# Two transformer blocks on one core: attention's products a stage later, earlier bias rows and squares, the last norm without GpSimd

## The chip, the core and the metric

The kernel runs on one core of a Trainium2 chip. The metric is device time of one execution in microseconds (us). The engines are named as the profile names them: PE (TensorE; PEld is its weight loads), DVE (VectorE), ACT (ScalarE), POOL (GpSimd) and SP (SyncE, which here issues nearly all DMAs).

## The reference

256 tokens of width 1024, fp32, go through two different transformer blocks and a last norm:

```python
# block 1
h = token_mixer(rmsnorm(x, norm_mix_pre), w_in, ...)      # four groups of 4 heads x 64:
#   mLSTM, short convolution, MoBA attention (one block of 256 keys: causal, with a relative bias),
#   HGRN2; head norms and gates; then y @ w_out
x = x + rmsnorm(h, norm_mix_post)
x = x + rmsnorm(memory_cross_attention(rmsnorm(x), rmsnorm(mem, mem_norm), ...))
x = x + rmsnorm(conv_glu_ffn(rmsnorm(x), ...))
# block 2
h = x + hybrid_mixer(rmsnorm_2(x, norm_mix), ...)  # 8 "fox" heads (causal, with a decay), 8 NSA heads
#   (compressed, selected and window branch), each 512 wide, up-projected, gated, summed, @ w_out
h = h + peer_ffn(rmsnorm_2(h, norm_ffn), ...)      # 16,384 single-neuron experts, top 16 of 8 heads
return rmsnorm_2(h, norm_final)                    # h * rsqrt(mean(h*h) + 1e-6) * norm_final
```

## The kernel before, in words

**Products.** The activations lie as features x tokens. Every weight and every activation is split into a high half (ACT copies it, L370) and a low half (the difference: DVE, or POOL for every so many weights, L328), and each product is three matmuls into one PSUM tile: `mm3`, L346 to 351, so that L349, L350 and L351 are the lines of nearly all of PE's work. `whalf` (L319) loads 512 KB of weights on SP's queue and makes both halves; four buffers of each are there. `fm_pair` makes 256 output features (48 matmuls), `fm_quad` (L390) two such pairs at once. PSUM has four tiles `acc` and four `att`.

**Order.** The program is written out stage by stage; a scheduler then orders each engine's instructions, except in pieces marked as ordered by hand. `behind()` and `issue_after` only add a constraint. Small attention work is written as generators, which `step()` or `next()` moves on by one stage between the big projections.

**Attention** (`attention`, L1673) is used three times: MoBA in block 1 (2 steps of two heads), fox (4 steps) and NSA (8 steps) in block 2. `scores` puts q·k and the biases into PSUM, ACT takes the exponentials, DVE the maxima, the sums' reciprocals and the scaling (L1710), and the result is `attP`. `values` transposes it on PE (L1718), ACT copies it to `attPT`, and PE multiplies it by v (L1726). A stage is: the scores of step j+1, then transposes and products of step j.

**Block 1's mixer** (L1354) makes the projections one by one and advances `moba`, `lstm` (mLSTM, L1532; two stages for each half c of the heads) and `memory` (keys and values of the memory, `memory_kv`, L649) between them. MoBA's bias comes from small tables: `cst1` and `bk` are loaded (L1513, L1514), a matmul (L1517) makes the rows `dr`, which go to DRAM and come back as the Toeplitz tile `toep` (L1522). Each half of mLSTM and HGRN2 ends in a `head_norm` (L555): square on ACT, a matmul for the means (L562), Ln and Exp on ACT, three DVE steps (`newton`, L450 to 452), a product with the gate on POOL (L567) and one on DVE (L569) into `y`. `y` is split into `yh` and `yl`, two of its eight rows of features at a time, and the mixer's output projection (`fm_quad` with the order 6, 7, 2, 3, 4, 5, 0, 1) multiplies those; rows 0 and 1 are mLSTM's. The memory's norm sums (squares on ACT, DVE additions, a matmul L470) are asked for by its first pair of projections.

**Block 2** (L762). `rotated` (L925) projects, rotates (a matmul, L864) and advances fox by one stage; `merge(j)` (L944) makes the gates' projections, one for each NSA stage. Between them lies a small softmax over compressed keys (L975 to L977), transposed at L981.

**Last norm** (L1312 to 1352, DVE and ACT ordered by hand). Two halves of 128 tokens by two halves of 512 features. `square` adds the last products (L1316), squares on ACT with a row sum and multiplies by the weights on POOL (L1319). `rms` and `newton` make the factor of a token half; `store` multiplies by it (DVE, L1337; ACT for the last quarter) and issues the DMA (three on SP, the last on ACT, L1338).

Of the kernel before, what the change touches and what calls it, by code (L numbers as in the profile page):

```python
# [15 lines left out]
AF = mybir.ActivationFunctionType  # L16
# [276 lines left out]
class Normed:  # L293


    def __init__(self, x, hi, lo):
        self.x, self.halves, self.r, self.rc, self.first = x, (hi, lo), None, None, None


class Prog:  # L300
# [68 lines left out]
    def act(self, out, in_, f, **k):  # L369
        return self.nc.scalar.activation(out, in_, f, **k)  # L370
# [83 lines left out]
    def norm_sums(self, n):  # L454

        if n.r is not None:
            return
        nc, x = self.nc, n.x
        s = None
        for p in range(4):  # L460
            sq = self.npool.tile([128, 2, T], F32, tag="sq" if s is not None else "sums", name="sq", bufs=3 if s is not None else 1)
            i = self.act(sq, x[:, 2 * p:2 * p + 2], AF.Square)
            if s is None:
                s = sq
                table = self.lntable(i)
            else:
                nc.vector.tensor_add(s, s, sq)
        ms = self.att((128, T))
# [180 lines left out]
    def memory_kv(self, pool, mem, km, vm):  # L649

        n = Normed(mem, *[pool.tile([128, 8, T], F32R, tag="mn" + t, name="mn" + t) for t in "hl"])
        self.norm_sums(n)
        self.gain_halves(n, self.v("mem_norm"))
        yield
        for j in range(2):
            ps = self.fm_norm(n, after=None)
            self.act(km[:, 2 * j:2 * j + 2].rearrange("p a b -> p (a b)"), ps, AF.Copy)
            yield
        ps = self.tm(n.halves, 512, self.plast)
        for b in range(2):  # L660
            self.act(vm[:, b], ps[b], AF.Identity, scale=self.cols(n, b))
# [100 lines left out]
    def block2(self, n):  # L762
# [4 lines left out]
        with tc.tile_pool(name="b2", bufs=1) as bp:  # L767
# [8 lines left out]
            with tc.tile_pool(name="b2a", bufs=1) as ap:  # L776
# [148 lines left out]
                def rotated(dst, scale):  # L925
                    r = rope(fl(dst), self.fm_pair(n.halves), T, c2("cosT"), c2("sinT"), scale)
                    next(r)
                    next(fox, None)
                    next(r, None)
                    next(cmp)  # L930
# [9 lines left out]
                for _ in fox:  # L940
                    pass
# [15 lines left out]
                merge(0)  # L957

# [19 lines left out]
                merge(1)  # L978
                pt = self.att((128, 2, 128))
# [3 lines left out]
                for j in range(2, 8):  # L983
                    next(nsa, None)
                    merge(j)
                for _ in nsa:
                    pass
                mr = self.npool.tile([128, 8, T], F32, tag="hg", name="mr")
                mh, ml = [ap.tile([128, 8, T], F32R, tag=t, name=t) for t in ("fqk", "knq")]
                for m_, y in ((0, yf), (1, yn)):  # L990
                    yh = ap.tile([128, 2, 4, T], F32R, tag="LR"[m_] + "T", name="yh")
                    for j in range(2):
                        self.split(yh[:, 0, 2 * j:2 * j + 2], yh[:, 1, 2 * j:2 * j + 2], y[:, 2 * j:2 * j + 2])
                    y = yh[:, 0], yh[:, 1]
                    for j in range(4):
                        ps = self.fm_pair(y, nk=4)
# [171 lines left out]
    def peer(self):  # L1168
# [7 lines left out]
        with ExitStack() as es:  # L1176
# [137 lines left out]

            def square(b, n):
# [17 lines left out]
            def store(b, n):  # L1333
                if b and n:
                    act(half[b][n], half[b][n], AF.Identity, scale=r[b])
                else:
                    nc.vector.tensor_scalar(half[b][n], half[b][n], r[b], None, op0=ALU.mult)  # L1337
                (nc.scalar if b and n else nc.sync).dma_start(self.out[b * 128:(b + 1) * 128, n * 512:(n + 1) * 512], half[b][n])  # L1338

            with tc.manual_schedule(engines={mybir.EngineType.DVE, mybir.EngineType.Activation}):  # L1340
                square(0, 0)
                square(0, 1)
                rms(0)
                square(1, 0)
                newton(0)
                square(1, 1)
                store(0, 0)
                store(0, 1)
                rms(1)
                newton(1)  # L1350
                store(1, 0)
                store(1, 1)

    def block1_mixer(self, n, first):  # L1354
# [4 lines left out]
        with tc.tile_pool(name="mix", bufs=1) as mp:  # L1359
# [143 lines left out]
            mq = proj("m_q")  # L1503
            mk = proj("m_k", 0.125, hb[:, 4:6])
            aq = proj("a_q", 0.125, hb[:, 6:8])
            ak = proj("a_k")
            values(512, 768)
            step(levels)

# [12 lines left out]
            nc.sync.dma_start(toep, bass.AP(tensor=dr.tensor, offset=dr.offset, ap=[[1, 128], [384, 4], [1, T]]))  # L1522

# [10 lines left out]
            def mlstm():  # L1534
                W = mp.tile([128, 4, 384], F32, tag="mW", name="mW")
                for c in range(2):
# [17 lines left out]
                    pn, pd, pm = [self.att((128, T)) for _ in range(3)]  # L1554
# [5 lines left out]
                    mm(pm, sel[:, 2 * c:2 * c + 2].rearrange("p h d -> p (h d)"), g4[:, 4], start=True, stop=True)  # L1560
                    em = v2("em")[:, :1]
# [31 lines left out]
            step(moba)  # L1593
# [25 lines left out]
            cc = proj("c_c")  # L1619
            step(lstm)  # L1620
# [4 lines left out]
            self.table = self.htable  # L1625
# [47 lines left out]
    def attention(self, pool, npair, q, k, v, bias, out, nsa=None):  # L1673
# [5 lines left out]

        nc, mm = self.nc, self.nc.tensor.matmul  # L1680
# [32 lines left out]
        def values(P, ch, br):  # L1713
# [7 lines left out]
            first = None  # L1721
            for blk in range(2):
                for i in (1, 0):
# [4 lines left out]
                    first = first or m  # L1728
# [3 lines left out]
        P = scores(*steps[0])  # L1732
        yield
        for j, step in enumerate(steps):
            p = step[0] // 2
            last, P = P, scores(*steps[j + 1]) if j + 1 < len(steps) else None
            if j % per == 0:
                po = self.acc((128, 2, T))
                if nsa:
                    for c in range(2):  # L1740
                        nsa[1](po, c, 2 * p + c)
            values(last, *step)
            if j % per == per - 1:
                nc.vector.tensor_copy(out[:, 2 * p:2 * p + 2], po)
            yield
# [22 lines left out]
```

## Time and profile before

| what | us |
|---|---|
| three runs: median (lowest to highest) | 1486.6 (1484.2 to 1488.93) |
| the profiled execution's own time | 1486.23 |
| its span, first to last instruction | 1484.5 |
| PE busy | 1439.0 (97%) |
| DVE busy | 1081.2 (73%) |
| ACT busy | 782.6 (53%) |
| POOL busy | 227.6 (15%) |
| mean granted TensorE clock | 0.995 of full speed |

The page gives busy times as shares of the span. PE's share hides its waits, which stand in the timeline of its instructions as "[idle before <-releaser]". By its timeline the stages are: block 1's mixer to about 180 us, the cross attention to about 270, the FFN, block 2's mixer from about 455 to 650, expert retrieval to 760, the experts to 1471, and the last norm.

### The profile page before, as it was taken

To read this page: it belongs to the slowest core of one execution; us is meant where nothing else is said; L and a number is where in the kernel's file an instruction comes from. 1 tells how busy PE (TensorE), PEld (TensorE's weight loads), DVE (VectorE), ACT (ScalarE), POOL (GpSimd) and SP (SyncE) were. 2 spreads that over 40 slices of the span, in tenths; PEclk is the share of its full clock that TensorE was granted. 3 is DMA by queue.
4 is the path that set the end of the run, shared out by engine and by line. 5 is a ranking of instruction groups with operands and counts; after the bars stand their busy time and mean duration, and the time that the engine had idled before them with its cause. 6 is when DMAs were issued, how large, how long until landed. Compare 5 with 4: busy or idle time off the path is not lost.

```text
span 1484.5 us, 26777 instructions
## 1 busy us (share of the span) xinstructions
PE 1439.0 (97%) x10614; PEld 1335.9 (90%) x10614; DVE 1081.2 (73%) x1994; ACT 782.6 (53%) x1314; POOL 227.6 (15%) x143
## 2 busy tenths in 40 slices
PE   8899898999999999999899999999999999999997
PEld 7789888999999889999899999999998888888886
DVE  7768687766777655579988888778887555655555
ACT  7446466444556756556444545544445455455454
POOL 3731000222200431106441220000000000000001
PEclk9999999999999999999999999999999999999999
DMA  6443332555555423464355545545446555655553
GB/s 245 149 158 127 126 117 93 176 175 185 194 172 176 157 90 125 128 199 164 122 183 163 167 157 185 166 162 170 159 167 217 197 192 192 198 194 191 196 191 123
DMA packets 68245, 246.64 MB, mean 166 GB/s; under 512 B 7540, under 2 KB 8568, under 8 KB 67864
## 3 DMA queue, kind: packets, MB, share of 16 engines
q1 hardware_dynamic: 67544, 243.10, 50.0%
q8 instruction: 83, 1.36, 0.4%
q10 hardware_dynamic: 576, 1.84, 0.3%
q14 instruction: 42, 0.34, 0.1%
HBM read 242.80 MB, written 2.10 MB: 165 GB/s over the span
## 4 chain that ended last, share of the span: by engine, by line
PE 74%; DVE 10%; ACT 2%; issue 1%; POOL 0%; ACTq 0%; DVEq 0%
PE acc L349 20%; PE acc L350 20%; PE acc L351 19%; PE att L350 3%; PE att L351 3%; PE att L349 3%; PE att L1240 2%; DVE wl L328 1%; DVE uvl L1094 1%; DVE tmp L1016 1%; PE att L1691 1%; PE acc L1726 1%; ACT wh L370 1%; DVE ti L1019 1%; DVE ti L1018 1%
## 5 line engine op out<-in xcount | busy, mean ns | idle before, releaser
L1094 DVE TENSOR_TENSOR uvl<-uv,uvh 128x1024 fp32r<-128x1024 f32 x234 | 291.7, 1247 | 153.9 <-ACT uvh L370 153.7
L370 ACT ACTIVATE uvh<-uv 128x1024 fp32r<-128x1024 f32 x256 | 270.2, 1057 | 237.0 <-PE acc L350 133.4
L370 ACT ACTIVATE wh<-w 128x1024 fp32r<-128x1024 f32 x187 | 195.9, 1056 | 200.9 <-PE acc L350 104.0
L351 PE MATMUL acc<-hh,uvl 128*128 128x256 f32 x1024 | 289.8, 283 | 5.3 <-DVE uvl L1094 4.3
L349 PE MATMUL acc<-hh,uvh 128*128 128x256 f32 x1024 | 294.2, 287 | 0.1
L350 PE MATMUL acc<-hl,uvh 128*128 128x256 f32 x1024 | 289.9, 283 | 0.0
L328 DVE TENSOR_TENSOR wl<-w,wh 128x1024 fp32r<-128x1024 f32 x146 | 184.6, 1272 | 76.6 <-ACT wh L370 76.0
L351 PEld LDWEIGHTS acc<-hh,uvl 128*128 128x128 f32 x1024 | 196.0, 191 | 6.1 <-DVE uvl L1094 4.9
L350 PE MATMUL acc<-uvl,ch 128*128 128x512 f32 x512 | 199.2, 389 | 0.0
L351 PE MATMUL acc<-uvh,cl 128*128 128x512 f32 x512 | 199.2, 389 | 0.0
L349 PEld LDWEIGHTS acc<-hh,uvh 128*128 128x128 f32 x1024 | 196.0, 191 | 0.3 <-ACT uvh L370 0.3
L350 PEld LDWEIGHTS acc<-hl,uvh 128*128 128x128 f32 x1024 | 196.1, 192 | 0.0
L349 PE MATMUL acc<-xnh,wh 128*128 128x256 f32 x544 | 156.9, 289 | 4.6 <-ACT wh L370 3.2
L328 POOL TENSOR_TENSOR wl<-w,wh 128x1024 fp32r<-128x1024 f32 x41 | 101.0, 2464 | 369.1 <-ACT wh L370 362.2
L351 PE MATMUL acc<-xnh,wl 128*128 128x256 f32 x544 | 155.0, 285 | 1.7 <-POOL wl L328 1.0
L350 PE MATMUL acc<-xnl,wh 128*128 128x256 f32 x544 | 155.4, 286 | 0.2
L349 PE MATMUL acc<-uvh,ch 128*128 128x512 f32 x512 | 138.5, 389 | 0.0
L349 PEld LDWEIGHTS acc<-uvh,ch 128*128 128x128 f32 x512 | 96.1, 188 | 20.0
L350 PEld LDWEIGHTS acc<-uvl,ch 128*128 128x128 f32 x512 | 96.1, 188 | 19.9
L351 PEld LDWEIGHTS acc<-uvh,cl 128*128 128x128 f32 x512 | 96.1, 188 | 19.9
L349 PEld LDWEIGHTS acc<-xnh,wh 128*128 128x128 f32 x544 | 104.2, 192 | 8.1 <-ACT wh L370 4.5
L350 PE MATMUL att<-xnl,wh 128*128 128x256 f32 x368 | 104.5, 284 | 2.9 <-DVE xnl L545 2.9
(433 smaller groups left out, 2959.3 us busy)
## 6 DMA issues: line engine op xcount, KB each, us to landing
w<-in_W_dram SPq DMA_DIRECT2D x188, 512.0 KB, 4.4
uv<-in_U_dram SPq DMA_DIRECT2D x128, 512.0 KB, 3.6
uv<-in_V_dram SPq DMA_DIRECT2D x128, 512.0 KB, 3.6
mg<-in_cw_dram SPq DMA_DIRECT2D x4, 512.0 KB, 7.2
x<-in_xT_dram SPq DMA_DIRECT2D x2, 512.0 KB, 5.4
mem<-in_memT_dram SPq DMA_DIRECT2D x1, 1024.0 KB, 6.6
sk<-in_W_dram SPq DMA_DIRECT2D x1, 1024.0 KB, 6.3
xd<-xt SPq DMA_DIRECT2D x2, 512.0 KB, 2.6
```

Source lines behind the costliest of these rows:

```text
L328: (self.nc.gpsimd if pool else self.nc.vector).tensor_tensor(out=lo, in0=w, in1=hi.bitcast(F32), op=ALU.subtract)
L349: mm(ps, wsl(w[0]), xsl(x[0]), start=first, stop=False, **k)
L350: mm(ps, wsl(w[0]), xsl(x[1]), start=False, stop=False, **k)
L351: self.last_mm = mm(ps, wsl(w[1]), xsl(x[0]), start=False, stop=last, **k)
L370: return self.nc.scalar.activation(out, in_, f, **k)
L1016: nc.vector.match_replace(tmp[:, :n], vals[:, 0:8], src, -3.0e38)
L1018: nc.vector.max_index(idx[:, 0:8], vals[:, 0:8], src)
L1019: nc.vector.max_index(idx[:, 8:16], vals[:, 8:16], tmp[:, :n])
L1094: i = (nc.gpsimd if lo_pool else nc.vector).tensor_tensor(out=lo, in0=w, in1=hi.bitcast(F32), op=ALU.subtract)
L1240: mm(ps[:, j], m1[:, j], m2[:, s * NT + j], start=s == 0, stop=s == 1)
L1691: m = mm(S[i][:, part[blk]], q[rows[i], ch, blk * 128:(blk + 1) * 128], k[rows[i], br if nsa else ch, :128 * (blk + 1)], start=blk == 1, s ...
L1726: m = mm(po[rows[i], ch % 2, 128 * blk:], v[:, blk, vc:vc + 64], PT[i][:, 256 * blk:256 + 128 * blk], start=not nsa and blk == 0, stop=blk ...
```

## The change

**Attention.** `values` is cut in two: `turn` transposes and copies, `values` multiplies. A stage now is either "products of step j-1, then scores of step j+1" or "transposes of step j", so a step takes two stages, and its products come behind the next step's scores. The callers step twice where they stepped once; the small softmax's transposes are moved behind `merge(2)`, and the last NSA stages go between the up-projections.

```diff
-        def values(P, ch, br):
+        def turn(P):
             PT = []
...
                 self.act(PT[i], pt, AF.Copy)
-            first = None
+            return PT
+
+        def values(PT, ch, br):
+            first = self.last_mm
...
-        for j, step in enumerate(steps):
-            p = step[0] // 2
+        for j in range(len(steps) + 1):
+            if j:
+                p = steps[j - 1][0] // 2
+                if j % per == 1:
+                    po = self.acc((128, 2, T))
...
+                values(PT, *steps[j - 1])
+                if j % per == 0:
+                    nc.vector.tensor_copy(out[:, 2 * p:2 * p + 2], po)
+            if j == len(steps):
+                return
             last, P = P, scores(*steps[j + 1]) if j + 1 < len(steps) else None
-            if j % per == 0:
...
-            values(last, *step)
...
+            yield
+            PT = turn(last)
             yield
```

**Block 1.** The bias rows (L1511 to 1522) stand ahead of the projections `m_q` to `a_v` instead of behind them. The memory's squares are cut out of `norm_sums` and asked for at the start of `memory_kv`; its sums are finished in mLSTM's second half. Two of mLSTM's PSUM tiles become one.

```diff
     def memory_kv(self, pool, mem, km, vm):
-        self.norm_sums(n)
+        self.squares(n)
         self.gain_halves(n, self.v("mem_norm"))
+        self.mem = n
...
-                    pn, pd, pm = [self.att((128, T)) for _ in range(3)]
+                    pq = self.att((128, 2, T))
+                    pn, pd = pq[:, 0], pq[:, 1]
+                    pm = self.att((128, T))
...
+                    if c:
+                        self.table = self.htable
+                        self.norm_sums(self.mem)
```

**Last norm.** The multiplication by the weights moves from POOL to DVE, for three of the four quarters, between the additions, into rows of a buffer that is free by then (`og`). The last quarter is stored by one DVE instruction that multiplies by both; ACT scales two quarters.

```diff
-                nc.gpsimd.tensor_tensor(out=half[b][n], in0=half[b][n], in1=gn[:, n * 512:(n + 1) * 512], op=ALU.mult)
+            def gained(b, n):
+                nc.vector.tensor_mul(og[b][n], half[b][n], gh[n])
...
+            def store(b, n, scalar):
+                o = og[b][n]
+                if scalar:
+                    act(o, o, AF.Identity, scale=r[b])
+                elif b and n:
+                    nc.vector.scalar_tensor_tensor(o, half[b][n], r[b], gh[n], op0=ALU.mult, op1=ALU.mult)
                 else:
+                    nc.vector.tensor_scalar(o, o, r[b], None, op0=ALU.mult)
```

PE and SP have as many instructions as before, DVE 2 more, ACT 1 more, POOL 4 fewer. Three places show the new order; line numbers are each kernel's own (1751 and 1762 are the new 1718 and 1726, 569 the new 562).

PE at the end of block 1's mixer (`yh`, `yl` the halves of `y`; `sq` mLSTM's squares, `attP` and `attPT` MoBA's), before:

```order
L351 MATMUL acc<-yh,wl 128x256
L562 MATMUL att<-sq,bd_128 128x256
L1718 MATMUL att<-ident,attP 128x128 x6
L1726 MATMUL acc<-attPT,vt 64x256 x2
L1726 MATMUL acc<-attPT,vt 64x128 x2
L349 MATMUL acc<-yh,wh 128x256 x2
L350 MATMUL acc<-yl,wh 128x256
```

and now (the two matmuls of L349 in one row are the first of rows 0 and 1 for both pairs there, as in the row above):

```order
L349 MATMUL acc<-yh,wh 128x256
L350 MATMUL acc<-yl,wh 128x256
L569 MATMUL att<-sq,bd_128 128x256
L351 MATMUL acc<-yh,wl 128x256
L349 MATMUL acc<-yh,wh 128x256 x2
L350 MATMUL acc<-yl,wh 128x256
```

MoBA's transposes and products are gone from between the head norm's matmul and the rows of `y` that come out of that head norm; they stand earlier.

PE in block 2 at the first fox step, before:

```order
L834 MATMUL att<-maskb,identb 128x128
L1718 MATMUL att<-ident,attP 128x128 x6
L864 MATMUL att<-raw,cst_5049 128x256 x2
L1726 MATMUL acc<-attPT,vt 64x256 x2
L1726 MATMUL acc<-attPT,vt 64x128 x2
L349 MATMUL acc<-xnh,wh 128x256
```

and now, around the first of the two groups of transposes (L1751; the products, L1762, stand 30 rows further down, behind the scores of the next step):

```order
L349 MATMUL acc<-xnh,wh 128x256
L872 MATMUL att<-raw,cst_5047 128x256 x2
L1751 MATMUL att<-ident,attP 128x128 x3
L350 MATMUL acc<-xnl,wh 128x256
L351 MATMUL acc<-xnh,wl 128x256
```

Big matmuls stand between scores, transposes and products, which followed each other directly before.

DVE at the end of the program (`fin` the result, `fss` and `fr` the sums and factors of a token half), before:

```order
L1316 TENSOR_TENSOR fin<-fin,acc 128x512
L1329 SCALAR_TENSOR_TENSOR fss_16431<-fss_16431,fr_16433 128x1
L1330 TENSOR_SCALAR fss_16431<-fss_16431 128x1
L1331 TENSOR_TENSOR fr_16433<-fss_16431,fr_16433 128x1
L1316 TENSOR_TENSOR fin<-fin,acc 128x512
L1337 TENSOR_SCALAR fin<-fin,fr_16433 128x512 x2
L1322 TENSOR_TENSOR fss_16432<-fss_16432 128x1
```

and now:

```order
L1334 TENSOR_TENSOR fin<-fin,acc 128x512
L1338 TENSOR_TENSOR buf_8313<-fin,gn 128x512
L1334 TENSOR_TENSOR fin<-fin,acc 128x512
L1348 SCALAR_TENSOR_TENSOR fss_16429<-fss_16429,fr_16431 128x1
L1349 TENSOR_SCALAR fss_16429<-fss_16429 128x1
L1350 TENSOR_TENSOR fr_16431<-fss_16429,fr_16431 128x1
L1341 TENSOR_TENSOR fss_16430<-fss_16430 128x1
L1343 TENSOR_SCALAR fss_16430<-fss_16430 128x1
L1359 TENSOR_SCALAR buf_8313<-buf_8313,fr_16431 128x512
```

The sums of the second token half (`fss_16430`) stand ahead of the first store; before, two stores stood ahead of them.

## Rows read from the trace of the kernel before

**Rows 1.** The page: busy us, share of the span and instructions of each engine.

```profile
PE 1439.0 (97%) x10614; PEld 1335.9 (90%) x10614; DVE 1081.2 (73%) x1994; ACT 782.6 (53%) x1314; POOL 227.6 (15%) x143
```

**Rows 2.** Timeline of PE in block 1: start us, us, instruction, [idle before <-releaser].

```profile
92.33 1.55 PE L1525 MATMUL att<-toep,cst 128*128 128x256 f32 x8 [0.88 <-DMA toep<-dr]
...
107.94 0.44 PE L1609 MATMUL att<-hA,vt 128*64 128x128 f32 x4 [1.52 <-ACT attPT L370]
...
152.54 0.39 PE L349 MATMUL acc<-yh,wh 128*128 128x256 f32 x1 [0.95 <-ACT km L370]
...
155.52 0.59 PE L562 MATMUL att<-sq,bd 128*128 128x256 f32 x2
...
157.80 0.87 PE L1726 MATMUL acc<-attPT,vt 128*64 128x256 f32 x8 [1.03 <-ACT attPT L370]
...
160.12 0.50 PE L349 MATMUL acc<-yh,wh 128*128 128x256 f32 x2 [1.46 <-ACT yh L370]
...
160.85 0.39 PE L350 MATMUL acc<-yl,wh 128*128 128x256 f32 x1 [0.22 <-DVE yl L341]
...
161.07 0.28 PE L351 MATMUL acc<-yh,wl 128*128 128x256 f32 x1
...
161.19 0.28 PE L349 MATMUL acc<-yh,wh 128*128 128x256 f32 x1
```

**Rows 3.** Windows: stretch, us, busy us (instructions) per engine, PEclk, DMA share, GB/s.

```profile
160.00:165.00 5.00, 4.65 (x24) 4.45 (x25) 1.49 (x3) 0.70 (x2) 0.00 (x0) 0.66 0.00 0
...
205.00:215.00 10.00, 7.34 (x40) 6.07 (x39) 7.20 (x13) 4.53 (x14) 0.00 (x0) 0.89 0.50 161
...
250.00:260.00 10.00, 6.46 (x46) 5.96 (x47) 8.01 (x15) 5.95 (x11) 2.13 (x1) 1.00 0.28 88
...
500.00:530.00 30.00, 28.26 (x279) 24.32 (x278) 19.20 (x42) 15.18 (x43) 11.72 (x8) 1.00 0.44 152
```

**Rows 4.** Timeline of PE, two of its other waits, in cross attention.

```profile
211.59 0.41 PE L691 MATMUL att<-ident,cP 128*128 128x128 f32 x2 [2.49 <-DVE cP L685]
...
258.24 1.13 PE L470 MATMUL att<-sq,onesd 128*128 128x256 f32 x4 [2.53 <-DVE sq L467]
```

**Rows 5.** Timeline of ACT, POOL, DVE between PE's rows at 155.52 and 160.85.

```profile
156.21 0.47 ACT L370 ACTIVATE sq<-att,epsc 128x256 f32<-128x256 f32 x1 [1.13 <-PE att L562]
...
156.58 0.48 ACT L370 ACTIVATE attPT<-att 128x384 f32<-128x384 f32 x1
...
158.94 0.73 POOL L567 TENSOR_TENSOR sq<-sq,mo 128x256 f32<-128x256 f32 x1 [16.52 <-DVE sq L452]
...
159.71 0.48 DVE L569 SCALAR_TENSOR_TENSOR y<-em,vec,sq 128x256 f32<-128x256 f32 x1 [0.30 <-POOL sq L567]
...
160.22 0.63 ACT L370 ACTIVATE yh<-y 128x512 fp32r<-128x512 f32 x1 [0.15 <-DVE y L569]
```

**Rows 6.** Timeline of PE in block 2's attention.

```profile
503.55 1.07 PE L1718 MATMUL att<-ident,attP 128*128 128x128 f32 x6 [1.06 <-DVE attP L1710]
...
527.69 1.13 PE L864 MATMUL att<-raw,cst 128*128 128x256 f32 x4 [0.31 <-ACT attPT L370]
...
555.33 0.44 PE L981 MATMUL att<-ident,L 128*128 128x128 f32 x2 [1.52 <-DVE L L977]
```

**Rows 7.** Timeline of DVE and ACT at the end of the program.

```profile
1472.81 0.69 DVE L1316 TENSOR_TENSOR fin<-fin,acc 128x512 f32<-128x512 f32 x1 [0.67 <-PE acc L351]
...
1475.94 0.68 DVE L1316 TENSOR_TENSOR fin<-fin,acc 128x512 f32<-128x512 f32 x1
...
1476.54 2.48 DVE L1337 TENSOR_SCALAR fin<-fin,fr 128x512 f32<-128x512 f32 x2
...
1480.40 0.49 DVE L1337 TENSOR_SCALAR fin<-fin,fr 128x512 f32<-128x512 f32 x1
...
1480.39 0.72 ACT L370 ACTIVATE fin<-fin,fr 128x512 f32<-128x512 f32 x1 [0.73 <-DVE fr L1331]
...
1481.14 0.34 ACTq L1338 DMA_DIRECT2D out_dram<-fin  x1
```

More of the change, by code (lines that the diff above doesn't have):

```diff
@@ L296, in __init__ @@
     def __init__(self, x, hi, lo):
-        self.x, self.halves, self.r, self.rc, self.first = x, (hi, lo), None, None, None
+        self.x, self.halves, self.r, self.rc, self.first, self.sums = x, (hi, lo), None, None, None, None
 class Prog:
@@ L452, in newton, with squares @@
         stt(r, q, 1.5, r, op0=ALU.add, op1=ALU.mult)
-    def norm_sums(self, n):
-        if n.r is not None:
-            return
+    def squares(self, n):
         nc, x = self.nc, n.x
@@ L463, in norm_sums @@
             if s is None:
-                s = sq
-                table = self.lntable(i)
+                s, n.last = sq, i
             else:
                 nc.vector.tensor_add(s, s, sq)
+        n.sums = s
+    def norm_sums(self, n):
+        if n.r is not None:
+            return
+        nc = self.nc
+        if n.sums is None:
+            self.squares(n)
+        s, table = n.sums, self.lntable(n.last)
         ms = self.att((128, T))
@@ L927, in rotated @@
                     next(r)
-                    next(fox, None)
+                    next(fox)
                     next(r, None)
+                    next(fox)
                     next(cmp)
@@ L939, in block2 @@
                 next(cmp)
-                for _ in fox:
-                    pass
+                for _ in range(2):
+                    next(fox)
                 def merge(j):
@@ L957, in block2 @@
                 merge(0)
+                for _ in fox:
+                    pass
                 L = ap.tile([128, 2, 4, 2, 16], F32, name="L")
@@ L978, in block2 @@
                 merge(1)
+                for _ in range(2):
+                    next(nsa)
+                merge(2)
                 pt = self.att((128, 2, 128))
@@ L982, in block2 @@
                 act(PC, pt.rearrange("p a b -> p (a b)"), AF.Copy)
-                for j in range(2, 8):
-                    next(nsa, None)
+                for j in range(3, 8):
+                    for _ in range(2):
+                        next(nsa)
                     merge(j)
-                for _ in nsa:
-                    pass
                 mr = self.npool.tile([128, 8, T], F32, tag="hg", name="mr")
@@ L995, in block2 @@
                     for j in range(4):
+                        for _ in range(2):
+                            next(nsa, None)
                         ps = self.fm_pair(y, nk=4)
@@ L1501, in proj @@
                 return t
[L1503 to L1508, printed above, removed]
             bk = mp.tile([32, 768], F32, tag="attP", name="bk", bufs=2)
@@ L1522, in block1_mixer @@
             nc.sync.dma_start(toep, bass.AP(tensor=dr.tensor, offset=dr.offset, ap=[[1, 128], [384, 4], [1, T]]))
+            mq = proj("m_q")
+            mk = proj("m_k", 0.125, hb[:, 4:6])
+            aq = proj("a_q", 0.125, hb[:, 6:8])
+            ak = proj("a_k")
+            values(512, 768)
+            step(levels)
             def moba_bias(S, h, blk, flags):
@@ L1592, in block1_mixer @@
                 pass
-            step(moba)
+            for _ in range(2):
+                step(moba)
             mem = self.npool.tile([128, 8, T], F32, tag="hg", name="mem")
@@ L1619, in block1_mixer @@
             cc = proj("c_c")
+            for _ in range(2):
+                step(moba)
             step(lstm)
@@ L1727, in values @@
                                start=not nsa and blk == 0, stop=blk == 1, skip_group_check=True)
-                    first = first or m
+                    first = m if blk == 0 and i else first
         steps = [(ch, br) for ch in range(2 * npair) for br in range(2 if nsa else 1)]
         per = len(steps) // npair
-        P = scores(*steps[0])
+        P, PT = scores(*steps[0]), None
         yield
-        for j, step in enumerate(steps):
-            p = step[0] // 2
-            last, P = P, scores(*steps[j + 1]) if j + 1 < len(steps) else None
-            if j % per == 0:
[L1738 to L1741, printed above, removed]
-            values(last, *step)
-            if j % per == per - 1:
-                nc.vector.tensor_copy(out[:, 2 * p:2 * p + 2], po)
+        for j in range(len(steps) + 1):
[3 more added lines that the diff above has]
+                    po = self.acc((128, 2, T))
+                    if nsa:
+                        for c in range(2):
+                            nsa[1](po, c, 2 * p + c)
+                values(PT, *steps[j - 1])
+                if j % per == 0:
+                    nc.vector.tensor_copy(out[:, 2 * p:2 * p + 2], po)
+            if j == len(steps):
+                return
+            last, P = P, scores(*steps[j + 1]) if j + 1 < len(steps) else None
+            yield
+            PT = turn(last)
             yield
```

23 lines of the change are left out of this document (12 added, 11 removed).

## The prediction

> **What bounds the kernel now.** I read the page first: PE is busy 1439.0 us, 97% of the span, and DVE, next in line, 73% [rows 1]. A change can therefore win only what PE waits for, what PE does slowly, and the end of the program, where PE has finished. So I went on to PE's timeline in the places that the diff touches, where each wait stands in brackets with its releaser, then to the windows for the granted clock, then to the other engines' timelines behind the longest waits. PE has waits of over 2 us elsewhere, in the cross attention for example [rows 4]; the change does not reach those.
>
> In block 1 the touched waits are 0.88 for the bias tile coming back from DRAM, 1.52 for an attPT copy, 0.95 for the memory's keys, 1.03 for another attPT copy, 1.46 for `yh` and 0.22 for `yl` [rows 2]: 6.06 us together. Behind the last two the granted clock falls: over 160 to 165 it is 0.66, part of that stretch at the lower of its two levels (1.2 GHz), and 4.65 busy us at 0.34 below full cost about 1.6 us [rows 3]. In block 2 they are 1.06 for `attP`, 0.31 for attPT and 1.52 for the compressed softmax `L` [rows 6]: 2.89 us. At the end PE is done and DVE sets the pace: the last addition runs at 1475.94, two stores take 2.48 us before the last token half's sums get their turn, and the last DMA is issued at 1481.14 [rows 7].
>
> **Bias rows earlier.** Same loads, same matmul, only sooner. The wait of 0.88 goes, since the round trip through DRAM now lies four projections ahead of its reader. On SP's queue the two tables pass a few weight loads, and `toep`'s load, which waits there for `dr`, stands in front of later weights. A weight tile feeds 24 matmuls at 0.12 us (161.07 to 161.19 [rows 2]), some 2.9 us, and four tiles are buffered, so a hold of that queue about as long as the wait of 0.88 is covered by the tiles ahead. If they are not ahead, one tile late costs up to its own 2.9 us. I take 0, with 0 to +2.9 as ends.
>
> **Block 1's attention and squares.** The order shows what MoBA's waits of 1.52 and 1.03 turn into: big projections now stand between transposes and products. The memory's squares come early, so its sums no longer stand in front of the keys (0.95). But MoBA's transposes and products also used to lie between mLSTM's head norm matmul and the first rows of `yh` made from it, and now only a few matmuls do. That chain is serial: from the matmul at 155.52 through Ln, Exp, DVE's three steps, POOL's product (158.94), DVE's (159.71) and ACT's copy, which starts at 160.22 and takes 0.63 [rows 2, 5]: 160.85 less 155.52 is 5.33 us. Without the attPT copy that delayed Exp (156.58 is where it starts; I allow 0.35 of its 0.48 [rows 5]) it is 5.0. PE covers about 0.65 of it: the norm's own matmul and the two or three that follow in the new order. So PE stands still for 4.35 us, in one piece, and then some 0.47 for `yl` (half of DVE's work behind `yh`, in place of 0.22). All six old waits, 6.06, are replaced by 4.82: -1.24.
>
> Against that stands interruption. A big matmul that follows another starts 0.12 later; after a small group or a wait it takes 0.22 (160.85 to 161.07 [rows 2]), so each return to the big stream costs some 0.1. In block 1 the order has 18 switches between small and big matmuls before and 33 now. That is 15 more, at 0.05 to 0.1 each: +0.75 to +1.5, and I take +1.1. Block 1 comes to -0.14. Its ends: if other work still hides the chain as it did, only about 2.5 us (the old 1.03 and 1.46) are left and the block wins 2.8; if the whole 5.33 is exposed and returns cost 1.5, it loses 1.2.
>
> **The clock.** In the trace of before, the waits of 0.95, 1.03 and 1.46 within nine us end in the fall to 0.66 described above [rows 2, 3]. In the cross attention a single wait of 2.49 ends in a window of clock 0.89, yet one of 2.53 stands in a window at 1.00 [rows 3, 4]. So a wait of this length may or may not lower the clock. I take the same fall as before, hence 0, with ends -1.6 (none) and +1.6 (twice as much low clock). The Trainium skill, "TensorE: Matmul & The Clock Gate", section "Why this matters for your kernels", speaks against this part of the change: long enough idle between matmul bursts puts the clock back to half, so that joining short gaps into a long one is the wrong direction. By that rule the sum would be higher by the second end; the rows agree at 211.59 and not at 258.24.
>
> **Block 2's attention.** Twelve steps (four fox, eight NSA) get big matmuls between transposes and products, and the compressed softmax's transposes move some 50 big matmuls (6 us at 0.12) behind where they waited 1.52. All 2.89 go. The order has 58 switches before and 50 now, so about 0.4 comes on top: -3.3. What is late next? attPT and `attP` have two buffers each, as before, and a step's products are issued before the next step's transposes write them. Ends: 0 (each wait comes back elsewhere) and -3.7.
>
> **Last norm.** Between the additions of the first quarters DVE waits for PE, 0.67 us at 1472.81, so the new multiplications of 0.68 (the price of the addition, same shape [rows 7]) nearly fit there, and the last addition, at 1475.94, no longer has the first half's DVE steps in front of it. The last addition ends at about 1476.5 either way; its square on ACT takes 0.72 by ACT's nearest row of that shape; the sums, Ln, Exp and three small DVE steps took 1.4 (the stores end at 1476.54 + 2.48 = 1479.02, the factor is used at 1480.39 [rows 7]); a store of 0.49 lies between; the last store takes 0.7. Together 1476.5 + 0.72 + 1.4 + 0.49 + 0.7 = 1479.8, against a DMA issue at 1481.14: -1.3. The DMAs themselves are the same four. Ends: -0.6 (three stores landing close together) and -1.7 (the store of 0.49 hidden beside Ln and Exp).
>
> **The sum.** -0.14 - 3.3 - 1.3 = -4.7. The profiled execution took 1486.23, close to the median of 1486.6, so the forecast is **1481.5**. Its own range, with the ends above adding partly: 1479 to 1484. About 0.3%, 4.5 us, is what a measurement of this kernel can tell from no change; against the median that is 1482.1.
>
> **Rivals.**
> (A) Block 1 gains too: the clock does not fall (-1.6) or part of the chain is hidden by rows of `y` (up to -2.7). For it: the second long wait of the cross attention costs no clock. Against it: the order leaves only two or three matmuls there. 1486.23 - 2.2 - 3.3 - 1.3 = 1479.4, down to 1477.5 with both.
> (B) The joined wait drops the clock for twice as long: +1.6 on the sum, 1483.1. For it: one long wait is what stands before the clock of 0.89 at 211.59. Against it: 258.24.
> (C) Block 2's attention gives nothing: the products are late again because a copy or the scaling comes a stage later too. Then 1486.23 - 0.14 - 1.3 = 1484.8. Against it: the big matmuls between them last longer than the copies of 0.48 [rows 5].
> (D) Slower. DVE cannot keep up when scores of step j+1 precede the transposes of step j: each of the twelve steps of block 2 waits for its scaling as the first fox step did, 1.06 [rows 6], 12.7 us in all: 1486.23 - 0.14 - 1.3 + 12.7 = 1497.5. It decides from the point where DVE's work for a step outlasts PE's between two transposes. For it: one step already waits. Against it: DVE is busy 19.20 of 30 us around fox [rows 3], and eleven of the twelve steps show no such wait before.
>
> **How the numbers follow.** Forecast 0.52, A 0.20, B 0.12, C 0.09, D 0.07. Of the forecast, two thirds lie below 1482.1. Faster by over 0.3%: 0.34 + 0.20 = 0.54. Within 0.3%: 0.18 + 0.12 + 0.09 = 0.39. Slower: 0.07. The range of 8 in 10 leaves out D and the far edges of A and C: 1478 to 1486.
>
> **What would show it.** Right: no wait for `toep`, for attPT, `attP` or `L`; one wait of 4 to 5 us in front of the last rows of `yh` at about 155 to 160, followed by a stretch of low clock; the last norm starting some 3 to 4 us earlier; and its last DMA issued some 4 us after the start of the last addition, where it was 1481.14 - 1475.94 = 5.2 [rows 7]. It would be wrong if that one wait were under 3 us or split (A), if twice as many matmuls behind it ran at the lower clock (B), or if waits on DVE or ACT stood before transposes and products of block 2 (C, D).

## The result and the profile after

Eight runs of the changed kernel have a median of 1479.72 us (1476.35 to 1482.89), eight of the kernel before, on the same chip, 1486.69 (1484.2 to 1489.33). The ratio is 0.9947, 95% interval 0.9932 to 0.9963: 7.0 us faster in the medians, where 4.7 were forecast. The profiled execution took 1478.34, with a span of 1476.6 against 1484.5.

On the page PE is as busy as before, 1437.5 us against 1439.0 in [rows 1], in a span shorter by 7.9:

```profile
PE 1437.5 (97%) x10614; PEld 1336.2 (90%) x10614; DVE 1079.0 (73%) x1996; ACT 782.2 (53%) x1315; POOL 223.3 (15%) x139
```

PE's waits by line and releaser (columns: engine, line and what it waited for; us in total, times, longest):

```profile
PE acc L349 <- ACT yh L370: 4.4, 1, 4.4
PE acc L351 <- DVE uvl L1109: 4.3, 3, 1.8
PE acc L349 <- ACT wh L370: 3.2, 2, 2.8
```

Nothing of attPT, `attP`, `L` or `toep` is left in that view; one wait for `yh` leads it. Where the time came from is read by putting the same instruction of both traces side by side:

| place on PE | before, us | after, us | difference |
|---|---|---|---|
| first means of the mixer's output (L508, now L515) | 179.86 | 179.79 | -0.07 |
| second fox scores (L1691, now L1724) | 497.36 | 497.34 | -0.02 |
| first output projection of block 2 (L350, `knq`) | 636.09 | 629.85 | -6.24 |
| last norm: last addition on DVE (L1316, now L1334) | 1475.94 | 1469.35 | -6.59 |
| end of the span | 1484.5 | 1476.6 | -7.9 |

So between these two executions block 1 is worth nothing, block 2's attention 6.2, the last norm 1.3. In block 1 the new wait stands in PE's timeline where [rows 2] had 1.03, 1.46 and 0.22, and behind it big matmuls start 0.21 apart, not 0.12, until 168:

```profile
162.75 0.80 PE L349 MATMUL acc<-yh,wh 128*128 128x256 f32 x2 [4.38 <-ACT yh L370]
163.47 0.58 PE L350 MATMUL acc<-yl,wh 128*128 128x256 f32 x1
163.85 0.42 PE L351 MATMUL acc<-yh,wl 128*128 128x256 f32 x1
164.07 0.41 PE L349 MATMUL acc<-yh,wh 128*128 128x256 f32 x1
```

The windows answer to those of [rows 3] (columns as there). The clock is low past 165, which it was not before; in fox's stretch PE is busy all of 30 us, where it had 28.26:

```profile
160.00:165.00 5.00, 2.25 (x9) 2.03 (x10) 1.78 (x4) 0.63 (x1) 0.72 (x1) 0.64 0.01 2
165.00:170.00 5.00, 5.00 (x32) 5.00 (x32) 3.15 (x4) 4.60 (x5) 0.00 (x0) 0.68 0.22 83
500.00:530.00 30.00, 30.00 (x301) 27.48 (x300) 20.54 (x49) 15.94 (x45) 14.18 (x9) 1.00 0.45 151
```

At the end, DVE and ACT, against [rows 7]: the last DMA is issued 3.64 us behind the start of the last addition, where it was 5.20. Nearly all of that 1.56 is gained ahead of the second token half's sums, which start 1.47 us behind that addition, where it was 3.01; from the sums to the DMA it is 2.17 and was 2.19. Before, with POOL's multiplications beside the stores:

```profile
1476.07 2.67 POOL L1319 TENSOR_TENSOR fin<-fin,gn 128x512 f32<-128x512 f32 x2 [0.44 <-ACT sq L370]
...
1478.95 0.15 DVE L1322 TENSOR_TENSOR fss<-fss 128x1 f32<-128x1 f32 x1
```

and now:

```profile
1469.35 0.68 DVE L1334 TENSOR_TENSOR fin<-fin,acc 128x512 f32<-128x512 f32 x1
...
1470.82 0.16 DVE L1341 TENSOR_TENSOR fss<-fss 128x1 f32<-128x1 f32 x1 [0.28 <-ACT sq L370]
...
1471.08 0.48 DVE L1359 TENSOR_SCALAR buf<-buf,fr 128x512 f32<-128x512 f32 x1
...
1472.21 0.75 DVE L1357 SCALAR_TENSOR_TENSOR buf<-fin,fr,gn 128x512 f32<-128x512 f32 x1
```

```profile
1472.99 0.35 ACTq L1360 DMA_DIRECT2D out_dram<-buf  x1
```

The two stores that stood ahead of the sums took 2.48 us while POOL was multiplying; a store of that shape took 0.49 before, once POOL was done [rows 7], and takes 0.48 now. How much of the 1.56 comes from the order and how much from POOL's absence, no run separates.

### The profile page after: what moved, and what is told of

Its sections match the earlier page's. It is cut to its first block, busy times and chain, and to the rows that moved or that the text cites. A ratio compares the mean times of both kernels' runs of the same rounds, so it can differ in the third digit from the quotient of the medians.

```text
span 1476.6 us, 26774 instructions
## 1 busy us (share of the span) xinstructions
PE 1437.5 (97%) x10614; PEld 1336.2 (90%) x10614; DVE 1079.0 (73%) x1996; ACT 782.2 (53%) x1315; POOL 223.3 (15%) x139
## 4 chain that ended last, share of the span: by engine, by line
PE 75%; DVE 9%; ACT 1%; issue 1%; POOL 0%; ACTq 0%; DVEq 0%
PE acc L349 20%; PE acc L350 20%; PE acc L351 20%; PE att L350 3%; PE att L351 3%; PE att L349 3%; PE att L1255 2%; DVE wl L328 1%; DVE uvl L1109 1%; PE att L1724 1%; PE acc L1762 1%; DVE ti L1033 1%; DVE tmp L1031 1%; PE att L1751 1%; ACT wh L370 0%
## 5 line engine op out<-in xcount | busy, mean ns | idle before, releaser
L349 PE MATMUL acc<-hh,uvh 128*128 128x256 f32 x1024 | 294.0, 287 | 0.0
L350 PE MATMUL acc<-hl,uvh 128*128 128x256 f32 x1024 | 289.9, 283 | 0.0
L350 PE MATMUL acc<-uvl,ch 128*128 128x512 f32 x512 | 199.2, 389 | 0.0
L350 PEld LDWEIGHTS acc<-hl,uvh 128*128 128x128 f32 x1024 | 196.1, 192 | 0.0
L349 PEld LDWEIGHTS acc<-hh,uvh 128*128 128x128 f32 x1024 | 196.0, 191 | 0.0
L349 PE MATMUL acc<-xnh,wh 128*128 128x256 f32 x544 | 157.3, 290 | 4.7 <-ACT wh L370 3.2
L350 PE MATMUL acc<-xnl,wh 128*128 128x256 f32 x544 | 155.1, 285 | 0.2
L349 PE MATMUL acc<-uvh,ch 128*128 128x512 f32 x512 | 138.5, 389 | 0.0
L350 PEld LDWEIGHTS acc<-uvl,ch 128*128 128x128 f32 x512 | 96.1, 188 | 19.9
L349 PEld LDWEIGHTS acc<-uvh,ch 128*128 128x128 f32 x512 | 96.1, 188 | 19.9
L349 PEld LDWEIGHTS acc<-xnh,wh 128*128 128x128 f32 x544 | 104.3, 192 | 8.3 <-ACT wh L370 3.8
L351 PEld LDWEIGHTS acc<-xnh,wl 128*128 128x128 f32 x544 | 104.6, 192 | 3.5 <-POOL wl L328 1.4
```

Source lines behind the costliest of these rows:

```text
L349: mm(ps, wsl(w[0]), xsl(x[0]), start=first, stop=False, **k)
L350: mm(ps, wsl(w[0]), xsl(x[1]), start=False, stop=False, **k)
L351: self.last_mm = mm(ps, wsl(w[1]), xsl(x[0]), start=False, stop=last, **k)
```

## The experiments

### One part of the change at a time

`b2_only`, `b1_only` and `tail_only` are the kernel before with the change's pieces for block 2, for block 1 and for the last norm alone; where one block keeps its attention, both versions of the function stand in the kernel:

```diff
-            moba = self.attention(mp, 1, aq, ak, vt[:, :, 512:], [moba_bias], y[:, 4:6])
+            moba = self.attention_old(mp, 1, aq, ak, vt[:, :, 512:], [moba_bias], y[:, 4:6])
```

is the line in `b2_only`; `b1_only` does the same for fox and NSA.

> Only block 2's attention is a stage deeper (fox and NSA, with the stages that call them); block 1 keeps its old attention, bias rows and squares, and the last norm is the old one. Theory 1 (the gain is made in block 2 itself): the stretch from the second fox scores (497.3 us) to the first output projection shrinks by 6.2 us, from 139.2 to 133.0, as in the changed kernel, and the time falls by 6 to 6.5 us. Rival (the gain in block 2 is half of that, as forecast, and block 1 brings the rest): the stretch shrinks by 3.3 and the time falls by 3 to 4.

Measured: ratio to the kernel before 0.9957 (0.9941 to 0.9973), medians 1481.72 and 1487.44. The stretch from the second fox scores to the first output projection took 132.6 us (499.75 to 632.37), where the kernel before took 138.7. Theory 1 holds: block 2 alone brings 6.1 in the trace, 5.7 in the medians.

> Only block 1's parts: MoBA's attention a stage deeper, bias rows earlier, the memory's squares earlier; block 2's attention and the last norm are the old ones. Theory 1: the old waits go, one wait of 4.4 us in front of the last rows of yh takes their place, the low clock behind it lasts some 5 us, and the end of the mixer stays where it was (0 within 0.3 us); the time is the same within 1 us. Rival: the block gains 2 to 3 us in the runs as a whole, where the profiled execution does not show it.

Measured: ratio 1.0004 (0.9983 to 1.0024), 1487.98 against 1487.44. The wait for `yh` is there with 4.4 us:

```profile
PE acc L349 <- ACT yh L370: 4.4, 1, 4.4
```

Block 1's part shows no gain in the runs either, against the rival; the interval still leaves room for up to 2.5 us.

> Only the last norm without GpSimd. Theory 1: PE's end stays, the end of the program comes 1.3 to 1.4 us sooner (the last DMA issued about 4.4 us behind the start of PE's last matmul where it was 6.0); a difference of that size is not to be told from 0 in the runs' times. Rival: with nothing changed ahead of it the old order of the stores was hidden beside the last products, and the end moves by less than 0.5.

Measured: ratio 0.9992 (0.9979 to 1.0006), not to be told from 1, as both expected. In the trace the last DMA is issued at 1479.32, 3.65 us behind the start of the last addition at 1475.67, as in the changed kernel, and 4.42 behind PE's last matmul (1474.90), as theory 1 expected; so the gain of 1.3 to 1.6 is there with nothing changed ahead of it.

### What block 2's 6.2 us are made of

The brackets of [rows 6] had 2.89 us, and the forecast 3.3 with fewer switches. Two runs take the parts singly. `l981` moves one stage of the kernel before:

```diff
                 merge(1)
+                merge(2)
                 pt = self.att((128, 2, 128))
...
-                for j in range(2, 8):
+                for j in range(3, 8):
```

> The kernel before with one stage moved: the transposes of the small softmax behind merge(2). Attention is as before. Theory 1 (the waits that the change removes in block 2 are worth what the start-to-start times say, 1.6 us here): the wait of 1.5 in front of that transpose goes and block 2 ends 1.5 to 1.7 us sooner. Rival (the wait comes back in front of the transposes of the next NSA step, which then follow the scores at once): under 0.5 us.

`fox_only` is `b2_only` with NSA's steps as before.

> The kernel before with fox's four steps a stage deeper; NSA, block 1 and the last norm as before. Theory 1: by start-to-start times of the kernel before, fox's waits are 1.22 (in front of the first transposes), 0.70 and 0.56 (behind transposes) and 0.3, 2.8 us in all; the stretch from the second fox scores to the first NSA scores shrinks by 2.4 to 3. Rival (fox's waits are worth the 1.4 us that the brackets showed): 1 to 1.5.

Measured, `fox_only`: to the first NSA scores, the end that was named, 44.3 us (506.86 to 551.19) against 45.6, so 1.2 less, the rival's number; but ten more big matmuls, 1.2 us at 0.12, stand ahead of that point here. With equal work, to the second NSA scores, it is 55.8 us (506.86 to 562.64) against 58.3, so 2.5 less, although its wait for `L` grew from 1.52 to 2.26. That fits theory 1 (2.4 to 3), but what it holds is not fox's waits alone: the first NSA step's scores, which were cut in two before (below), are whole in this run. The waits alone are seen in the start-to-start times behind masks, transposes and rotations: summed up to the first NSA scores, these fall by 2.7, close to theory 1's 2.8. In `l981` the wait is gone, and 96 big matmuls run through at 0.12 each in front of the transposes:

```profile
565.02 0.38 PE L982 MATMUL att<-ident,L 128*128 128x128 f32 x2
565.33 0.92 PE L1692 MATMUL att<-kr,knq 64*128 64x256 f32 x8
```

But block 2 as a whole did not end sooner: 139.5 us against 138.7. The scheduler cut a second step of scores there, at 614.44 and 616.08, and in this execution the clock fell to 0.70 behind the first fox step's wait. For the block theory 1 failed; the rival's "under 0.5" came out, but not by its reason, since no wait stands in front of the next transposes. For the wait itself theory 1 was right. Each of the two kernels ran once, in 1492.59 and 1494.77 us, with granted clocks of 0.989 and 0.987; single times like these do not tell the parts apart.

The cut of a step came up in `solo_rows`, which changes only the order of a step's scores in the changed kernel:

```diff
-            order = [(blk, i) for blk in (1, 0) for i in (1, 0)]
+            order = [(blk, i) for i in (1, 0) for blk in (1, 0)]
```

> The changed kernel with the matmuls of each attention step's scores (q x k, and the biases added to them) in the order head 1, head 1, head 0, head 0, where the two heads alternated. Same instructions. Theory 3 (two matmuls that use different halves of PE's rows run beside each other when they follow each other; a step of scores that the scheduler had cut in two, 0.85 us for each half where an uncut one takes 0.85 in all, cost the kernel before about 1 us): each of the 14 steps takes 0.4 to 0.85 us longer on PE, 6 to 12 us in all, with no wait in the timeline. Rival (the cut step was slow for another reason, such as records missing from the trace): less than 2 us.

Measured: ratio 0.9948 (0.9931 to 0.9966), like the changed kernel's. The rival's number is right and its reason is not. PE's timeline (x counts two passes of each fp32 matmul) shows the first NSA step, cut by the scheduler into the two heads, and then a whole one:

```profile
547.36 0.92 PE L1724 MATMUL att<-kr,knq 64*128 64x256 f32 x4
...
548.72 0.92 PE L1724 MATMUL att<-kr,knq 64*128 64x256 f32 x4
...
558.32 0.93 PE L1724 MATMUL att<-kr,knq 64*128 64x256 f32 x8
```

Four matmuls last as long as the two of one head, in both orders in which they were written (in which order PE got them, the views do not show); what costs time is other work between the heads. The same stretch of block 2 is 133.7 us here (504.27 to 637.95) and 132.5 in the changed kernel, 1.2 more with one cut step. The kernel before had one too, the changed kernel none:

```profile
542.92 0.92 PE L1691 MATMUL att<-kr,knq 64*128 64x256 f32 x4
...
544.28 0.92 PE L1691 MATMUL att<-kr,knq 64*128 64x256 f32 x4
...
545.13 0.87 PE L1726 MATMUL acc<-attPT,vt 128*64 128x256 f32 x8
```

Its second half alone takes 0.85 to the next start, so a cut step costs 0.85 to 1.2.

The rest is in the brackets themselves. PE's rows of the kernel before around the first fox step:

```profile
502.09 0.40 PE L834 MATMUL att<-maskb,identb 128*128 128x128 bf16 x4
503.55 1.07 PE L1718 MATMUL att<-ident,attP 128*128 128x128 f32 x6 [1.06 <-DVE attP L1710]
504.83 1.10 PE L864 MATMUL att<-raw,cst 128*128 128x256 f32 x4 [0.21 <-ACT attPT L370]
```

From the masks to the transposes are 1.46 us, and in the changed kernel, where nothing is waited for, 0.24 (551.12 to 551.36); six transposes take 1.28 to the next start there and 0.57 here:

```profile
551.12 0.40 PE L842 MATMUL att<-maskb,identb 128*128 128x128 bf16 x4
551.36 0.82 PE L1751 MATMUL att<-ident,attP 128*128 128x128 f32 x6
```

So the waits of 1.06 and 0.21 were worth 1.22 and 0.70: a bracket counts from the modelled end of the instruction ahead, a start-to-start time from what PE could have done. Summed in that way, [rows 6]'s three waits and that of 0.21 are 1.22, 0.70, 0.56 and 1.6: 4.1. With the cut step's 0.85 to 1.2 that leaves 0.9 to 1.3 of 6.2 for fewer switches and a wait of 0.16 at 506.09; that rest was not measured by itself.

### The parts of block 1

`bias_late` and `sq_late` undo one piece each in the changed kernel: the bias rows behind the projections again, and

```diff
-        self.squares(n)
+        self.norm_sums(n)
...
-                    if c:
-                        self.table = self.htable
-                        self.norm_sums(self.mem)
...
+            self.table = self.htable
```

> The changed kernel with the bias rows back behind the projections m_q to a_v. Theory 1: the wait for toep comes back in front of MoBA's first bias matmul, 0.9 to 2.1 us, and the mixer's end comes about as much later; nothing else moves. Rival (the wait at the end of the mixer is set by DVE and ACT, not by PE, and swallows it): toep's wait is back but the wait in front of yh is shorter by as much, and the mixer ends where it does now.

Measured: the wait is back, a little smaller than expected, and the stretch from HGRN2's scores (`hqk`) at 48 us to the means at 179 is 130.6 us (48.03 to 178.63) where the changed kernel, run again, took 130.1 (48.82 to 178.91). The wait for `yh` is 4.38, unchanged:

```profile
90.69 1.55 PE L1550 MATMUL att<-toep,cst 128*128 128x256 f32 x8 [0.77 <-DMA toep<-dr]
```

So theory 1: it isn't swallowed, and the earlier bias rows bring 0.5 to 0.8 by themselves in this run. Where the bias rows are late, the same wait differs between executions: 0.70 in `b2_only`, 0.88 in the kernel before, 1.26 in `l981`, 3.11 in `fox_only`, and 2.11 in `tail_only`:

```profile
PE att L1535 <- DMA toep<-dr: 2.1, 1, 2.1
```

So 0.5 to 0.8 is the low end of what moving them can save.

> The changed kernel with the memory's squares and sums back in one piece, ahead of its first projections, as in the kernel before; attention stays a stage deeper. On PE mLSTM's second half's products then stand 55 rows later than in the changed kernel, behind the memory's sums and directly ahead of the last rows of y. Theory 1: the head norm's matmul itself waits about 1 us, the wait in front of yh stays at 4 to 4.5 us, and the mixer ends 0.5 to 2 us later than in the changed kernel. Rival (the squares' move gives nothing): the mixer ends within 0.3 us.

Measured: the head norm's matmul waits 2.16, the last rows of `yh` 4.50, and the means at the end stand at 181.07, where the changed kernel's first trace, with the same wait of 3.04 at 48 us, has 179.79.

```profile
159.50 0.70 PE L569 MATMUL att<-sq,bd 128*128 128x256 f32 x2 [2.16 <-ACT sq L370]
164.70 0.79 PE L349 MATMUL acc<-yh,wh 128*128 128x256 f32 x2 [4.50 <-ACT yh L370]
```

Theory 1 holds for the loss, 1.1 to 1.3 us (the head norm's own wait is longer than the 1 us expected); by these traces, with attention a stage deeper and the squares left where they were, block 1 would be slower than before.

### The wait that the change made

The new wait's chain in the changed kernel, ACT first:

```profile
154.62 0.40 ACT L370 ACTIVATE sq<-em 128x256 f32<-128x256 f32 x1
...
158.29 0.47 ACT L370 ACTIVATE sq<-att,epsc 128x256 f32<-128x256 f32 x1 [0.18 <-PE att L569]
...
162.06 0.63 ACT L370 ACTIVATE yh<-y 128x512 fp32r<-128x512 f32 x1 [2.85 <-DVE y L576]
```

mLSTM's squares end at 155.02, but PE comes to the head norm's matmul (L569) at 157.66, because it stands 34 rows behind the memory's sums (L477, at 152.72), among matmuls on `y`. `hold6` puts both earlier:

```diff
-        for k, p in steps:
-            for c in range(2):
+        for i, (k, p) in enumerate(steps):
+            with self.behind(hold.get(i)):
+                for c in range(2):
...
-            ps = self.fm_quad((hi, lo), order, 4)
+            ps = self.fm_quad((hi, lo), order, 4, {0: self.mlast, 6: self.hlast})
```

> The changed kernel with two matmuls put earlier on PE by an order constraint: the memory's norm sums ahead of the first matmul on y, and mLSTM's head norm matmul ahead of the seventh step of the output projection (so some 36 matmuls earlier). Theory 2 (the wait of 4.4 us in front of yh is a matter of order: the squares were ready 2.9 us before PE came to the head norm's matmul, because ACT stood behind the memory's sums): the wait shrinks from 4.4 to under 1 us, no stretch at the lower clock follows, and the kernel gains 4 to 6 us on the changed one. Rival (the chain waits for DVE, whose queue is full there): the head norm's matmul itself waits 3 to 4 us and nothing is gained.

Measured: ratio to the kernel before 0.9935 (0.9915 to 0.9956), 1476.19 us. By the ratios that is 1.8 us faster than the changed kernel (0.9947), with overlapping intervals, so the 4 to 6 us are not shown. The wait is 1.32, not under 1, and the clock still falls behind it (0.67 over 160 to 165). The head norm's matmul waits only 0.17, so the rival falls. What remains stands on ACT: the memory's key copies run at 153.08, and the head norm's Ln comes after them, although its matmul started at 152.08.

```profile
152.08 0.70 PE L570 MATMUL att<-sq,bd 128*128 128x256 f32 x2 [0.17 <-ACT sq L370]
...
158.64 0.50 PE L349 MATMUL acc<-yh,wh 128*128 128x256 f32 x2 [1.32 <-ACT yh L370]
```

```profile
153.08 1.20 ACT L370 ACTIVATE km<-acc 128x512 f32<-128x512 f32 x2 [1.05 <-DVE acc L412]
154.17 0.47 ACT L370 ACTIVATE sq<-att,epsc 128x256 f32<-128x256 f32 x1
```

`hold6k` turns those two round:

```diff
-        self.act(r, r, AF.Exp, scale=-0.5)
+        self.hexp = self.act(r, r, AF.Exp, scale=-0.5)
...
-            self.act(km[:, 2 * j:2 * j + 2].rearrange("p a b -> p (a b)"), ps, AF.Copy)
+            with self.behind(self.hexp):
+                self.act(km[:, 2 * j:2 * j + 2].rearrange("p a b -> p (a b)"), ps, AF.Copy)
```

> The kernel of the run hold6 with one more order constraint: ACT copies the memory's keys behind the Exp of the head norm, not ahead of its Ln (in hold6 the head norm's matmul ended about 152.7 us and ACT came to its Ln at 154.17, because two key copies of 1.20 us in all stood first). Theory 2 (what is left of the wait in front of yh, 1.3 us, is this queue): the wait falls to about 0.1 to 0.3 us, and with it the stretch at the lower clock gets shorter or goes; 1 to 2.5 us faster than hold6. Rival: the copies hold the PSUM tiles of the output projection, a wait of 1 us or more stands in front of another matmul, and nothing is gained.

Measured: ratio 0.9912 (0.9889 to 0.9936), 1476.83 us, which is not told from `hold6`: the intervals overlap and the median is no lower. The wait in front of `yh` is gone, 0.22 are left for `yl`, and the clock stays up:

```profile
160.00:165.00 5.00, 4.78 (x38) 4.39 (x37) 1.63 (x3) 2.18 (x3) 0.35 (x1) 1.00 0.01 2
165.00:170.00 5.00, 4.63 (x38) 4.42 (x38) 4.34 (x6) 4.97 (x7) 0.00 (x0) 1.00 0.55 179
```

The changed kernel and this version were then run again, side by side.

> The changed kernel once more, unedited, beside the version of the next run on the same chip. Theory (the executions of one kernel differ by several us because the clock falls in some of them behind some waits and not in others): its median is again 6 to 8 us under the kernel before, with a spread of 5 us or more. Rival: the change's gain belongs to that chip and day, and is under 4.5.

> The kernel of the run hold6k once more: the changed kernel with three order constraints at the end of block 1's mixer. Theory 2: no wait in front of yh and no low clock behind it, so 4 to 6 us faster than the changed kernel in the median, 10 to 13 under the kernel before. Rival (the first comparison flattered it): within 3 us of the changed kernel.

Measured: 0.9930 (0.9909 to 0.9950) and 0.9912 (0.9891 to 0.9933), medians 1476.97 and 1475.81, against 1487.87. The change's gain is there again, 10.9 us this time, more than expected; the version's lead is 1.2 in the medians, the rival's number, and the two intervals overlap. By the traces its stretch is shorter: from mLSTM's last products to the mixer's means the changed kernel takes 33.2 and 33.1 us (146.62 to 179.79, 145.86 to 178.91), `hold6` 30.0, `hold6k` 27.8 both times. Where the rest of those 5.3 us goes in the whole time is not settled: both traces of `hold6k` have a lower clock from 50 to 60 us (0.50 and 0.53, 0.52 and 0.80 in two windows of 5 us) than the changed kernel's two (0.79 and 1.00, 1.00 in both), ahead of anything that it changes. By these windows that is 4.9 and 3.4 us of PE's time against 1.1 and none, much of what is missing. `b1_only`, which has none of the constraints, shows 0.50 and 0.55 there, so it does not take them; that it is chance is likely but not shown. Neither `hold6` nor `hold6k` is shown to be faster than the changed kernel.

## Why the prediction was right

The sum of -4.7 had the right sign, and the median of 1479.72 lies inside the range of 1479 to 1484, 0.7 us above its lower end. That it lies inside is partly luck: the profiled execution, 1478.34, which is what the sum describes, lies below the range, and so does the median of 1476.97 when the changed kernel ran again. Block 2's term alone makes the difference. Step by step:

- **Block 1's chain.** Forecast: one wait of 4.35 us; measured: 4.38. Its parts are right too: 157.66 to the end of ACT's copy at 162.69 is 5.03, where 5.0 were forecast. The block's net of -0.14 came out as -0.07, and as 1.0004 in `b1_only`. The wait for `yl`, forecast at 0.47, has no bracket on PE, but it did not go: the weight load of that matmul waits, and the matmul starts 0.72 behind the first of `yh`, as before (0.73).

```profile
163.47 0.29 PEld L350 LDWEIGHTS acc<-yl,wh 128*128 128x128 f32 x1 [0.22 <-DVE yl L341]
```

- **The clock.** Taken as unchanged, with +1.6 as an end; it was wrong toward that end. In the windows, 2.25 busy us at 0.64 and 5 at 0.68, most of the big matmuls up to 168 started 0.21 apart, which is 1.2 GHz. By the windows, 0.36 of 2.25 and 0.32 of 5 are 2.4 us against 1.6 before (somewhat low, since the first window's 0.64 counts idle time at full clock). So what the rival (B) said happened in part in this pair of executions. The Trainium skill ("TensorE: Matmul & The Clock Gate", "Why this matters for your kernels") has the rule that long idle between matmul bursts puts the clock back to half; this pair agrees with it, 0.64 behind the wait of 4.38. Other executions do not bear the comparison out: by the same windows the joined wait of 4.38 cost 2.5 in `again` but 1.5 in `b1_only`, and the three old waits cost 2.9 in `l981`. What the joined wait costs in clock beyond the old ones is thus not settled; with no wait left (`hold6k`) the clock stayed at 1.00. The block came out even: -6.06 for the old waits, +4.38, +0.8 for the clock and a net of -0.07 leave 0.8, where I had 1.1 for the switches. As these are brackets, which block 2 showed to be too small, that rest is no measurement of the switches.
- **The bias rows.** Taken at 0 beside the wait of 0.88: no weight came late, and undoing it costs 0.5 to 0.8 in the one run that does.
- **Block 2's attention: the mis-sized term.** "All 2.89 go ... -3.3" was the step that failed in size: 6.2, and 6.1 alone, where its own end was -3.7. All waits went, as said, but each was larger than its bracket, 4.1 in all with one that I had left out, and one step's scores, cut in two by the scheduler, cost 0.85 to 1.2, which no wait in any view shows.
- **The last norm.** -1.3 forecast; the last store's DMA comes 1.56 sooner behind the last addition, the end 1.3, since the span now ends 3.6 us behind that issue, not 3.4. The store of 0.48 lies beside Ln and Exp (1471.08), as in the end of -1.7.
- **Rival D** (a wait in each of the twelve steps): none is there. DVE is busy 20.54 of 30 us around fox, and the matmuls between scores and transposes cover it. **Rival C** fell with `b2_only`. In **rival A** "both" comes to 1477.2 by its own terms, not 1477.5.

## What to carry to other kernels

Price a wait by the time from start to start against the same pair of instructions where nothing is waited for; the brackets here were only its lower part. Where a serial chain on three engines is exposed, look first at which queue each link stands in: here the matmul and then the Ln each stood behind work that was not urgent, and three order constraints took a wait of 4.4 us away, though the runs' times show at most a small part of it. Parts of a change that each free a wait may only trade it for another; the trace of each part alone shows which.

## What the runs showed of the hardware

- Two heads' scores use one half of PE's rows each, and when they follow each other they run beside each other: 0.85 us for four matmuls, 0.85 for the two of one head alone.
- The clock falls behind some waits in one execution and not in the next: behind the wait of 2.53 at 258 us it is 1.00 over 255 to 265 in the kernel before, and in `tail_only`, behind the same wait, 0.84 and 0.82 in the two windows of 5 us. Of the eight runs of the changed kernel the four up to 1479.22 us had a mean granted clock of 0.993 or 0.994, the four from 1480.22 on 0.990 or 0.991: much of a spread of 6.5 us goes with it. Not all does: in `again` an execution of 1475.55 and one of 1482.63 both have 0.992. `fox_only`, at 0.987, had low stretches at 50, 100, 165, 220, 265 and 890 us, of which the kernel before shows the first, the third and the fourth; the one at 100 comes behind a wait of 3.11 for `toep`, where the kernel before had 0.88.
